# Low parts of 18 up-projection chunks: an adding DMA onto a negated copy in place of VectorE's subtraction

## The chip, the cores and the metric

The kernel runs on one core of a Trainium2 chip. The metric is device time in microseconds (us) of one execution. Before the change two timed runs gave 581.53 and 582.05 us, median 581.79.

## The reference, cut to what matters

One decoder layer on 256 tokens of width 1024, all in float32:

```python
x = layer_norm(ALPHA * x + 0.5 * swiglu(x, w_gate1, w_up1, w_down1))   # FFN 1, width 2816
h = x @ w_in + b_in                                                    # queries, keys, values, gates
y = [mixer_b(h) @ w_proj_b for b in ("sliding window", "block sparse", "memory")]
x = layer_norm(ALPHA * x + sum(sigmoid(g_b) * y_b) @ w_out)
x = layer_norm(ALPHA * x + 0.5 * swiglu(x, w_gate2, w_up2, w_down2))   # FFN 2
# swiglu(x, g, u, d) = (silu(x @ g) * (x @ u)) @ d
```

Every weight is used once per execution, so the kernel streams all of them from device memory.

## The kernel before, in words

The weights are cut into chunks of 1 MiB, each a tile `raw` of [128, 2048] float32. By `plan()` there are 96 chunks (the short description of the change says 108): 33 for each FFN, 10 for the projections of the attention, 20 for gates, output projections and `w_out`. In an FFN the gate and up chunks alternate, g0, u0, g1, u1, ... g10, u10, and the 11 down chunks follow. In FFN 1 chunk number 2c is gate c and number 2c + 1 is up c. So "chunk 5" is the up chunk c = 2, and "chunk 21" is u10.

TensorE multiplies with two parts of every number, both in the format float32r: the high part `whi` is the rounded weight, the low part `wlo` is what is missing, `raw - whi`. `split` makes them, and every chunk goes through it:

```python
def split(src, hi, lo):
    nc.scalar.copy(hi, src)                                  # L125, ScalarE
    return nc.vector.tensor_sub(lo, src, hi.bitcast(F32))    # L126, VectorE
```

Three sets of tiles carry a chunk. `raws` has 3 buffers: the load of a later chunk waits until the last reader of the buffer is done. `parts` has 4 buffers for `whi` and 4 for `wlo`: the parts of chunk i go where chunk i - 4 was, so ScalarE can begin with chunk i when TensorE has finished chunk i - 4. TensorE's sums stand in 8 banks of `ps`, two for each gate or up chunk.

For a gate or up chunk `feature_tile_2` (L201, L202) runs, for each of two halves of 128 features, 8 pairs of matmuls: `whi` against 512 columns (both parts of x side by side), then `wlo` against 256. `added` (L207, L208) copies one half of the result with ScalarE (`b`) and adds the other with VectorE into `g` or `u`. After an up chunk `gated` takes the silu on ScalarE (`s`, L342) and the product on VectorE (`h`, L344), and `split` turns it into `hh` and `hl`.

Between the chunks of FFN 1 two hooks load other inputs. The second one, at c = 7, loads `memT` (1 MiB) into a `raw` buffer and splits it as well.

The order on ScalarE, VectorE, TensorE and GpSimd is set by the scheduler of the framework from data dependences and its own estimates, and on SP (the queue that issues the loads) it is the order of the program. Each engine works through its instructions in that order, and one that waits holds up those behind it. `queue_behind` adds orderings by hand: the VectorE pieces in `lows[i]` of some chunks issue after a named instruction of the layer norms, one of them for the up chunk c = 2 of FFN 2.

Below, T5 is the time at which TensorE begins chunk 5 of FFN 1, and so on.

Of the kernel before, what the change touches and what calls it, by code (L numbers as in the profile page):

```python
# [31 lines left out]
# columns of w_in  # L32
# [3 lines left out]
def plan():  # L36
    """The weights in the order of their use, in chunks of 1 MiB: key, how it is split, and the layout
    of its [128, 2048]. All but v and the rows of down and out are 8 row tiles of 256 columns."""
# [31 lines left out]
    # query heads i and 3 + i of a share a tile  # L70
# [19 lines left out]
def vectors(d):  # L90
    """Biases by partition: 3 pairs of query heads of a, keys of a, queries and keys of b, queries of m,
    gates, keys of mem; and those by column: sinks, values of a and b, values of mem."""
    b = d["b_in"][0]
    qa = b[QA : QA + 384].reshape(2, 3, 64).transpose(1, 0, 2).reshape(3, P)
    parts = [qa, b[KA : KA + P], b[QB : QB + 768], b[QM:], d["b_mem_kv"][0, :256]]
    by_partition = np.concatenate([v.reshape(-1, P) for v in parts]).T
    by_column = np.concatenate([d["attn_sinks"][0], b[VA : VA + P], b[VB : VB + 384], d["b_mem_kv"][0, 256:]])
    return by_partition, by_column[None]


class Parts(tuple):
    """The high and the low part of a [128, tiles, 2, tokens]"""
# [7 lines left out]
def hybrid_layer(ctx: ExitStack, tc: tile.TileContext, a: dict, out: bass.AP):  # L110
# [12 lines left out]
    def split(src, hi, lo):  # L123
        """src = hi + lo exactly, both of 12 significant bits"""
        nc.scalar.copy(hi, src)  # L125
        return nc.vector.tensor_sub(lo, src, hi.bitcast(F32))  # L126

    def queue_behind(ins, others):
        """others issue after ins, on the same engine"""
        for o in others:  # L130
            tc.add_manual_dep(o.ins, ins.ins.name, mybir.DependencyInfo(mybir.DependencyClass.NoSync,
                                                                        mybir.DependencyReason.DATA))

    # ---------------------------------------------------------------- weights
# [15 lines left out]
    def part_to(n):  # L150
        while done["part"] <= min(n, len(chunks) - 1):
            i = done["part"]
            load_to(i)
            raw, how = raw_of.pop(i), chunks[i][1]
            if how:
                t = "1" if how == "leadg" else "2"
                hi = acts.tile([P, 2048], F32R, name="lhi", tag="A" + t)
                lo = acts.tile([P, 2048], F32R, name="llo", tag="B" + t)
            else:
                hi = parts.tile([P, 2048], F32R, name="whi")  # L160
                lo = parts.tile([P, 2048], F32R, name="wlo")
            # in small pieces where the engines have other work to do in time
            n_ = 512 if i < 6 or index["mk"] - 4 <= i <= index["u", 2, 3] else 2048
            lows[i] = [split(raw[:, o : o + n_], hi[:, o : o + n_], lo[:, o : o + n_]) for o in range(0, 2048, n_)]
            part_of[i] = (hi, lo)
            done["part"] += 1
# [10 lines left out]
    def product(ps, terms, first=True, last=True):  # L177
        """ps = sum of l.T @ r over terms, each a pair of parts; low times low lies below float32"""
# [14 lines left out]
    def feature_tile(ps, w, col, x, n=KD):  # L193
        """ps [128 features, 256 tokens] of a chunk's columns"""
        product(ps, [(two(w, ALL, slice(k * 256 + col, k * 256 + col + P)), two(x, ALL, k, ALL)) for k in range(n)])

    def feature_tile_2(ps, w, col, x, ks=range(KD)):
        """ps [128 features, 2 x 256 tokens], whose halves add up to the product"""
# [5 lines left out]
    def added(dst, ps):  # L204
        """dst = the sum of the halves"""
# [4 lines left out]
    def token_tile(ps, w, x, t):  # L210
        """ps [tokens of tile t, the chunk's 256 columns]"""
        product(ps, [(two(x, ALL, k, tok(t)), two(w, ALL, slice(k * 256, (k + 1) * 256))) for k in range(KD)])

    # -------------------------------------------------------------- constants
# [15 lines left out]
    def tokens_of(name):  # L230
        """both parts side by side: a product can take them in one pass"""
# [6 lines left out]
    def transposed(src, t, dst, pool=mm):  # L238
        """src [128 tokens, 1024] -> both parts [128, 8, 256 tokens], at the tokens of tile t"""
# [8 lines left out]
    def keep_warm(n):  # L248
        """the tensor engine's clock rises, and stays up, while it has work"""
# [4 lines left out]
    # x and the first two chunks, split in the order in which they come  # L254
# [28 lines left out]
    def distances():  # L283
        # Out of sight where the mask is. Query tile 0 against keys 0-127,
        # query tile 1 against keys 0-255.
# [11 lines left out]
    # ------------------------------------------------------------------- FFN  # L297
    def halves(name, tags):
        """22 feature tiles of 256 tokens, in two tiles"""
# [5 lines left out]
    def per_token(keys, lhs, keep, after, ahead=2, between=None, ends=HALVES):  # L305
        """after(t, [(start, stop, columns)]) of lhs(k, t).T @ the row tiles of weights, 2 in a chunk. The
        last keep chunks are taken by token tile, so that tile 0 ends early, and the last two by columns:
        by halves, and for tile 1 by ends."""
# [30 lines left out]
    def gated(g, u):  # L339
        """half of silu(g) * u: the layer adds half of what the FFN gives"""  # L340
# [6 lines left out]
    def ffn(n, x, after, start=0, hooks={}, h=None, ends=HALVES):  # L347
        hh, hl = h or (halves("hh", ("A1", "A2")), halves("hl", ("B1", "B2")))
        for c in range(start, NC):
# [3 lines left out]
            for key in ("g", "u"):  # L353
                w = weights((key, n, c))
                ps = [mm.tile([P, 512], F32, name="ps") for _ in range(2)]
                # the first chunks by quarters, as they come
# [11 lines left out]
    # ------------------------------------------------------------ layer norms  # L368
# [6 lines left out]
    def normalize(t, pss, resid, put, k=1.0):  # L375
        """layer norm of alpha * resid + ps / k, by the columns of pss"""
# [30 lines left out]
    # --------------------------------------------------------- FFN 1 and LN 1  # L407
# [18 lines left out]
    # keys [128 of two heads, pair, 256] and values [128 keys, key tile, heads * 64] of mem  # L426
# [3 lines left out]
    def biased(ps, bc, hi, lo):  # L430
        """hi + lo = ps + bias, by partition"""
# [23 lines left out]
    # ------------------------------------------------------------ projections  # L455
    # feature tiles of two heads: B1 q and k of b, B2 q of a, k of a, q of m
# [6 lines left out]
    # what attention gives takes the place of its queries  # L463
# [21 lines left out]
    # -------------------------------------------------------------- attention  # L485
    # A head's scores: columns 0-127 are query tile 0 against keys 0-127, the
    # rest query tile 1 against all keys. Memory: query tiles against 256 keys.
# [6 lines left out]
    def scores(nm):  # L494
        """8 times the scores, and their softmax"""
# [4 lines left out]
        for e in range(0, n, 2):  # L500
            # two heads in turn, in the two halves of the rows
# [44 lines left out]
    def turn(nm, i):  # L546
        """the probabilities of a pair's heads with keys on partitions: keys 0-127, then 128-255"""
# [14 lines left out]
    def weigh(nm, i):  # L562
        """values [128 keys, two heads] against the probabilities of both"""
# [12 lines left out]
    # Twice a sigmoid is 1 + tanh of half its argument: the gates hold the tanh,  # L576
    # mixed is twice what the layer mixes, and the layer norm halves the sum.
# [51 lines left out]
    # ------------------------------------------------------ mix, W_out, LN 2  # L629
# [35 lines left out]
    # ----------------------------------------------------------- FFN 2, LN 3  # L665
    # The first chunks by token tile, so that tile 0 runs while tile 1 is normalized.
# [61 lines left out]
```

## Time and profile before

| | |
|---|---|
| timed runs | 581.53 and 582.05 us, median 581.79 us |
| span of the profiled execution (first to last instruction) | 580.4 us |
| what a timed run has beyond that span | 1.1 to 1.7 us |
| TensorE (PE) busy | 569.9 us, 98% of the span |
| VectorE (DVE) busy | 393.0 us, 68% |
| ScalarE (ACT) busy | 305.1 us, 53% |
| GpSimd (POOL) busy | 23.5 us, 4% |
| DMA engines busy, mean of 16 | some 52% of the span |

Busy time says how much work an engine had, not whether it set the end. A matmul's busy time overlaps with that of its neighbours. The profile names what ended each wait of an engine, and the chain of work that ended last; both are read below for the stretches that the change touches.

### The profile page before, as it was taken

The numbers are of one execution on the slowest core, as the hardware profiler recorded it, in microseconds if no ns is written. First come the engines' busy times: TensorE is split into PE (matmuls) and PEld (weight loads), VectorE is DVE, ScalarE is ACT, GpSimd is POOL, SyncE is SP. The second block draws the span as 40 slices with busy tenths as digits, with TensorE's granted clock in tenths as the row PEclk, the third lists the DMA queues.
The fourth block names the chain that finished last, engine by engine and source line by source line (L and its number), as shares of the span: only waits on it lengthen the run. The fifth ranks groups of instructions, "written<-read, shape, count | busy, mean of one in ns | idle before, by whom it ended". The sixth has DMA issues, their size and how long they took to land.

```text
span 580.4 us, 9070 instructions
## 1 busy us (share of the span) xinstructions
PE 569.9 (98%) x3634; PEld 514.3 (89%) x3634; DVE 393.0 (68%) x594; ACT 305.1 (53%) x528; POOL 23.5 (4%) x37
## 2 busy tenths in 40 slices
PE   8999999999999999999999999999999999999994
PEld 7888888888888998999999999889988888888884
DVE  5877667665446977698887566995557666663336
ACT  6865656644433653965965454633565645543300
POOL 2000000000000000000002012210000000000001
PEclk9999999999999999999999999999999999999998
DMA  8895747745543384094162554537454545546101
GB/s 274 313 322 226 272 152 289 265 164 217 213 165 131 146 290 145 14 350 147 62 230 88 204 212 151 217 146 256 180 177 186 213 154 213 194 169 218 73 0 72
DMA packets 18025, 108.99 MB, mean 188 GB/s; under 512 B 2112, under 2 KB 2368, under 8 KB 5696
## 3 DMA queue, kind: packets, MB, share of 16 engines
q1 hardware_dynamic: 17984, 108.43, 51.6%
q8 instruction: 28, 0.46, 0.3%
q14 instruction: 13, 0.11, 0.1%
HBM read 107.37 MB, written 1.05 MB: 187 GB/s over the span
## 4 chain that ended last, share of the span: by engine, by line
PE 93%; ACT 3%; DVE 2%; DMA 1%; issue 0%; POOLq 0%; SPq 0%; DVEq 0%
PE ps L201 25%; PE ps L182 18%; PE ps L181 18%; PE ps L183 17%; PE ps L202 13%; ACT whi L125 1%; DMA raw<-in_w_dram 1%; ACT sc_b L531 1%; PE ps L555 1%; PE ps L244 1%; DVE sc_b L515 0%; DVE m L520 0%; PE ps L508 0%; ACT gates L589 0%; DVE r L399 0%
## 5 line engine op out<-in xcount | busy, mean ns | idle before, releaser
L126 DVE TENSOR_TENSOR wlo<-raw,whi 128x512 fp32r<-128x512 f32 (+1 forms) x232 | 233.3, 1039 | 134.1 <-ACT whi L125 133.7
L125 ACT CAST whi<-raw 128x512 fp32r<-128x512 f32 (+1 forms) x232 | 196.2, 888 | 143.9 <-PE ps L183 58.3
L201 PE MATMUL ps<-x0T,whi 128*128 128x512 f32 x352 | 123.4, 396 | 1.2 <-ACT whi L125 0.7
L201 PE MATMUL ps<-x2T,whi 128*128 128x512 f32 x288 | 100.2, 394 | 0.0
L202 PE MATMUL ps<-x0T,wlo 128*128 128x256 f32 x352 | 97.9, 282 | 0.0
L181 PE MATMUL ps<-x1T,whi 128*128 128x256 f32 x288 | 82.3, 286 | 0.3 <-ACT sc_m L531 0.3
L182 PE MATMUL ps<-x1T,whi 128*128 128x256 f32 x288 | 81.5, 283 | 0.0
L183 PE MATMUL ps<-x1T,wlo 128*128 128x256 f32 x288 | 81.5, 283 | 0.0
L201 PEld LDWEIGHTS ps<-x0T,whi 128*128 128x128 f32 x352 | 66.4, 190 | 16.1 <-ACT whi L125 2.1
L202 PE MATMUL ps<-x2T,wlo 128*128 128x256 f32 x288 | 79.9, 277 | 0.0
L182 PE MATMUL ps<-wlo,hh 128*128 128x512 f32 (+1 forms) x198 | 72.5, 366 | 0.0
L181 PE MATMUL ps<-whi,hh 128*128 128x512 f32 (+1 forms) x198 | 72.5, 366 | 0.0
L183 PE MATMUL ps<-whi,hl 128*128 128x512 f32 (+1 forms) x198 | 72.4, 365 | 0.0
L202 PEld LDWEIGHTS ps<-x0T,wlo 128*128 128x128 f32 x352 | 67.2, 191 | 0.6
L201 PEld LDWEIGHTS ps<-x2T,whi 128*128 128x128 f32 x288 | 54.0, 188 | 12.6
L181 PEld LDWEIGHTS ps<-x1T,whi 128*128 128x128 f32 x288 | 55.2, 192 | 0.8 <-ACT sc_m L531 0.5
L182 PEld LDWEIGHTS ps<-x1T,whi 128*128 128x128 f32 x288 | 55.2, 192 | 0.0
L183 PEld LDWEIGHTS ps<-x1T,wlo 128*128 128x128 f32 x288 | 55.2, 192 | 0.0
L202 PEld LDWEIGHTS ps<-x2T,wlo 128*128 128x128 f32 x288 | 54.1, 188 | 0.0
L181 PEld LDWEIGHTS ps<-whi,hh 128*128 128x128 f32 x198 | 37.3, 188 | 6.2
L183 PEld LDWEIGHTS ps<-whi,hl 128*128 128x128 f32 x198 | 37.3, 188 | 6.1
L182 PEld LDWEIGHTS ps<-wlo,hh 128*128 128x128 f32 x198 | 37.3, 188 | 6.0
(167 smaller groups left out, 715.1 us busy)
## 6 DMA issues: line engine op xcount, KB each, us to landing
raw<-in_w_dram SPq DMA_DIRECT2D x92, 1024.0 KB, 4.8
raw<-in_w_dram SPq DMA_DIRECT2D x16, 256.0 KB, 5.4
ln<-in_ln_dram SPq DMA_DIRECT2D x3, 1024.0 KB, 6.8
xT<-in_xT_dram SPq DMA_DIRECT2D x4, 256.0 KB, 6.6
x_sb<-in_x_dram SPq DMA_DIRECT2D x1, 1024.0 KB, 7.1
raw<-in_memT_dram SPq DMA_DIRECT2D x1, 1024.0 KB, 5.2
out_dram<-r SPq DMA_DIRECT2D x3, 256.0 KB, 2.0
brow<-in_by_column_dram SPq DMA_DIRECT2D x1, 387.0 KB, 8.0
```

The source lines that it names most:

```text
L125: nc.scalar.copy(hi, src)
L126: return nc.vector.tensor_sub(lo, src, hi.bitcast(F32))
L181: nc.tensor.matmul(ps, lh, rh, start=first and i == 0, stop=False)
L182: nc.tensor.matmul(ps, lh, rl, start=False, stop=False)
L183: nc.tensor.matmul(ps, ll, rh, start=False, stop=last and i == n - 1)
L201: nc.tensor.matmul(ps, wh, x.both[:, k], start=k == 0, stop=False)
L202: nc.tensor.matmul(ps[:, S:], wl, x[0][:, k], start=False, stop=k == KD - 1)
L244: nc.tensor.transpose(ps[:, j * P : (j + 1) * P], src[:, k * P : (k + 1) * P], ident)
L531: nc.scalar.activation(sc[:, e, c0:c1], raw[e][:, c0:c1], AF.Exp, bias=negm[:, e, t : t + 1], scale=SCALE, accum_out=ssum[:, e, t : t + 1])
L555: nc.tensor.transpose(pt[:, s * n + j * P : s * n + (j + 1) * P], sc[:, 2 * i + s, c : c + P], ident)
```

## The change: what it does

For the up chunks with c from 2 to 10 of both FFNs (18 chunks) the low part is made in another way. ScalarE writes `whi` as before, in one piece of 2048 columns, then a second time the negated, rounded weight into `wlo`. GpSimd then issues a DMA that adds `raw` onto `wlo`, so that `wlo` ends as `raw - whi`. VectorE has no part in it. The list `lows` of such a chunk is empty, so the ordering by hand for the up chunk c = 2 of FFN 2 is gone. The diff without changes to comments:

```diff
-            n_ = 512 if i < 6 or index["mk"] - 4 <= i <= index["u", 2, 3] else 2048
-            lows[i] = [split(raw[:, o : o + n_], hi[:, o : o + n_], lo[:, o : o + n_]) for o in range(0, 2048, n_)]
+            key = chunks[i][0]
+            if key[0] == "u" and key[2] >= 2 and not how:
+                nc.scalar.copy(hi, raw)
+                nc.scalar.activation(lo, raw, AF.Copy, scale=-1.0)
+                nc.gpsimd.dma_start(out=lo, in_=raw, accum_op=ALU.add)
+                lows[i] = []
+            else:
+                n_ = 512 if i < 6 or index["mk"] - 4 <= i <= index["u", 2, 3] else 2048
+                lows[i] = [split(raw[:, o : o + n_], hi[:, o : o + n_], lo[:, o : o + n_]) for o in range(0, 2048, n_)]
```

In the rows that follow, a name ends in the number of its buffer, and the line numbers after the change are 8 higher from `split`'s callers on. First ScalarE's queue where chunk 5 (`raw_197`) is split, before and after; `raw_199` is chunk 6, `raw_252` chunk 7.

```order
L207 COPY b_361<-ps_324 128x256
L125 CAST whi_366<-raw_197 128x512 x4
L207 COPY b_411<-ps_376 128x256
L125 CAST whi_425<-raw_199 128x2048
L207 COPY b_414<-ps_377 128x256
L342 ACTIVATE s_417<-g_357 128x512
L125 CAST whi_472<-raw_252 128x2048
```

```order
L215 COPY b_361<-ps_324 128x256
L165 CAST whi_366<-raw_197 128x2048
L166 ACTIVATE wlo_367<-raw_197 128x2048
L215 COPY b_406<-ps_371 128x256
L125 CAST whi_420<-raw_199 128x2048
L215 COPY b_409<-ps_372 128x256
L350 ACTIVATE s_412<-g_357 128x512
L165 CAST whi_467<-raw_252 128x2048
L166 ACTIVATE wlo_468<-raw_252 128x2048
```

The four casts of chunk 5 have become one cast and the negated copy, back to back; chunk 7 has its negated copy behind its cast.

Next ScalarE's queue at an up chunk in the middle of FFN 1, chunk 15 (`raw_693` before, `raw_690` after); the copies `b` around it are those of chunks 13 and 14.

```order
L207 COPY b_834<-ps_799 128x256
L125 CAST whi_895<-raw_693 128x2048
L207 COPY b_837<-ps_800 128x256
L342 ACTIVATE s_840<-g_786 128x512
L207 COPY b_887<-ps_852 128x256
L125 CAST hh0_181<-h_842 128x512
```

```order
L215 COPY b_833<-ps_798 128x256
L165 CAST whi_894<-raw_690 128x2048
L215 COPY b_836<-ps_799 128x256
L350 ACTIVATE s_839<-g_784 128x512
L166 ACTIVATE wlo_895<-raw_690 128x2048
L125 CAST hh0_181<-h_841 128x512
L215 COPY b_886<-ps_851 128x256
```

The negated copy stands behind the copy `b` and the silu that follow the cast, and ahead of `hh`.

Last ScalarE's queue at the end of FFN 1's up chunks: `raw_892` is chunk 19, `raw_947` is `memT`, `raw_951` chunk 20, `raw_998` chunk 21. Only the queue after the change is shown; before it, the cast of `memT` stood ahead of the cast of chunk 19.

```order
L165 CAST whi_1101<-raw_892 128x2048
L215 COPY b_1043<-ps_1006 128x256
L350 ACTIVATE s_1046<-g_991 128x512
L166 ACTIVATE wlo_1102<-raw_892 128x2048
L125 CAST memT0_176<-raw_947 128x2048
L125 CAST hh1_182<-h_1048 128x512
L215 COPY b_1093<-ps_1058 128x256
L125 CAST whi_1155<-raw_951 128x2048
L215 COPY b_1096<-ps_1059 128x256
L215 COPY b_1141<-ps_1106 128x256
L215 COPY b_1144<-ps_1107 128x256
L350 ACTIVATE s_1147<-g_1092 128x512
```

The cast of `memT` has moved behind the negated copy of chunk 19; the cast of chunk 21, two `hh` and `b` instructions and its negated copy follow the last of these rows. On GpSimd nine DMA instructions now stand between the building of the distance tables and the first layer norm, and nine more between the second and the third. On SP the load of `memT` waits for the adding DMA of chunk 17, and the load of chunk 21 for VectorE's part of `memT`, whose buffer it takes.

## Rows read from the trace of the kernel before

**Rows 1.** The page: an engine's busy time and share; the granted clock in 40 slices.

```profile
PE 569.9 (98%) x3634; PEld 514.3 (89%) x3634; DVE 393.0 (68%) x594; ACT 305.1 (53%) x528; POOL 23.5 (4%) x37
PEclk9999999999999999999999999999999999999998
```

**Rows 2.** Busy time by stretch: length, then each engine; clock, DMA share, GB/s.

```profile
41.75:52.84 11.09, 11.09 (x66) 9.78 (x65) 7.31 (x8) 6.16 (x8) 0.00 (x0) 1.00 0.47 182
63.94:130.50 66.56, 66.56 (x386) 58.69 (x385) 45.94 (x49) 38.66 (x50) 0.00 (x0) 1.00 0.61 221
416.00:516.00 100.00, 100.00 (x578) 87.39 (x577) 65.06 (x71) 55.55 (x72) 0.00 (x0) 1.00 0.53 190
```

**Rows 3.** Waits of all engines: who waited for whom, total, times, longest.

```profile
DVE wlo L126 <- ACT whi L125: 133.7, 73, 5.7
...
ACT whi L125 <- PE ps L201: 44.1, 20, 2.6
...
PEld ps L201 <- ACT whi L125: 2.1, 2, 1.4
```

**Rows 4.** ScalarE in order of time, 26 to 37 us: start, length, what, wait before.

```profile
26.36 0.37 ACT L207 COPY b<-ps 128x256 f32<-128x256 f32 x1
26.62 2.19 ACT L125 CAST whi<-raw 128x512 fp32r<-128x512 f32 x4
...
29.41 1.91 ACT L125 CAST whi<-raw 128x2048 fp32r<-128x2048 f32 x1 [0.34 <-DMA raw<-in_w_dram]
...
36.20 1.92 ACT L125 CAST whi<-raw 128x2048 fp32r<-128x2048 f32 x1 [0.77 <-PE ps L201]
```

**Rows 5.** ScalarE in order of time, two chunks in the middle of FFN 1.

```profile
41.75 1.91 ACT L125 CAST whi<-raw 128x2048 fp32r<-128x2048 f32 x1 [2.22 <-PE ps L201]
43.56 0.36 ACT L207 COPY b<-ps 128x256 f32<-128x256 f32 x1
43.82 0.63 ACT L342 ACTIVATE s<-g 128x512 f32<-128x512 f32 x1
...
52.84 1.91 ACT L125 CAST whi<-raw 128x2048 fp32r<-128x2048 f32 x1 [2.28 <-PE ps L201]
```

**Rows 6.** VectorE in order of time at the same place.

```profile
43.69 2.29 DVE L126 TENSOR_TENSOR wlo<-raw,whi 128x2048 fp32r<-128x2048 f32 x1 [2.58 <-ACT whi L125]
45.90 0.42 DVE L208 TENSOR_TENSOR u<-ps,b 128x256 f32<-128x256 f32 x1
46.42 0.69 DVE L344 SCALAR_TENSOR_TENSOR h<-u,s 128x512 f32<-128x512 f32 x1
```

**Rows 7.** The page's DMA issues: transfer, queue, count, size, median us from issue to landing.

```profile
raw<-in_w_dram SPq DMA_DIRECT2D x92, 1024.0 KB, 4.8
```

**Rows 8.** DMA view, 74 to 107 us: GB/s in 40 slices.

```profile
GB/s 0 60 278 417 417 99 0 159 60 437 447 179 10 0 0 149 308 427 447 417 447 397 387 417 367 50 0 0 79 209 407 457 219 199 387 467 308 447 407 219
```

**Rows 9.** SP's queue in order of time: the load of memT.

```profile
90.39 0.33 SPq L419 DMA_DIRECT2D raw<-in_memT_dram  x1
```

**Rows 10.** ScalarE in order of time, 95 to 120 us.

```profile
95.62 1.92 ACT L125 CAST memT<-raw 128x2048 fp32r<-128x2048 f32 x1 [0.68 <-DMA raw<-in_memT_dram]
...
108.31 1.91 ACT L125 CAST whi<-raw 128x2048 fp32r<-128x2048 f32 x1 [2.22 <-PE ps L201]
...
110.38 0.63 ACT L342 ACTIVATE s<-g 128x512 f32<-128x512 f32 x1
...
113.71 0.62 ACT L125 CAST hh<-h 128x512 fp32r<-128x512 f32 x1 [2.13 <-DVE h L344]
114.23 0.37 ACT L207 COPY b<-ps 128x256 f32<-128x256 f32 x1
...
119.40 1.91 ACT L125 CAST whi<-raw 128x2048 fp32r<-128x2048 f32 x1 [2.28 <-PE ps L201]
```

**Rows 11.** VectorE in order of time: its part of memT.

```profile
97.57 2.29 DVE L126 TENSOR_TENSOR memT<-raw,memT 128x2048 fp32r<-128x2048 f32 x1 [0.68 <-ACT memT L125]
```

**Rows 12.** ScalarE in order of time, the start of FFN 2's up chunks.

```profile
395.79 1.07 ACT L125 CAST x2T<-ps 128x512 fp32r<-128x512 f32 x2
...
416.14 1.91 ACT L125 CAST whi<-raw 128x2048 fp32r<-128x2048 f32 x1 [2.37 <-PE ps L201]
```

## The prediction

> **What bounds the kernel now.** I began with the busy times and the granted clock [rows 1]. TensorE is busy 569.9 of the span's 580.4 us, at the full of its two clock levels in all but the last slice. A busy share is an average, so the next view was the busy time by stretch, for the gate and up chunks that the change touches [rows 2]: there TensorE is busy 11.09 of 11.09 us, 66.56 of 66.56 and 100.00 of 100.00. It never waits; two chunks take 11.09 us, one 5.55. VectorE has 7.3 us of work in those 11.09, ScalarE 6.2. The waits say the same from the other side [rows 3]: VectorE waits 133.7 us in all for ScalarE's casts, ScalarE 44.1 us for TensorE to free a buffer of parts, and the one wait of weight loading for a cast is 2.1 us, at the start. So the work that the change takes away stands beside a full TensorE, and the question is only whether the low parts still come in time.
>
> The time lines give the dates for that. ScalarE's cast of chunk i waits for TensorE to end chunk i - 4, so the casts that end a wait for TensorE mark borders between chunks: T5 = 36.20 [rows 4], T6 = 41.75 and T8 = 52.84 [rows 5], T18 = 108.31 and T20 = 119.40 [rows 10]; the rest follow at 5.55 us, T21 = 124.95 among them. In the middle of FFN 1 the cast of chunk 9 starts at T6 and VectorE's part ends at 43.69 + 2.29 = 45.98 [rows 6]; TensorE wants it at T9 = 58.4, 12.4 us later. That cover is what the change spends.
>
> **VectorE's part that goes.** 18 chunks at 2.29 us [rows 6], 41 us, all of it behind TensorE: 0 on the path. No gain hides there: TensorE's whole idle time is 580.4 - 569.9 = 10.5 us, and in the stretches concerned it is none [rows 2].
>
> **ScalarE's part that comes.** 18 passes over 2048 columns at 1.91 us, the price of the cast [rows 5]. Per pair of chunks ScalarE goes from 6.2 to 8.1 of 11.1 us. The copies behind it come up to 2 us later, which the 8 banks cover (a chunk takes two). If that cover were gone, a pass would cost its 1.91 us. On the path to the low part it counts in full.
>
> **The adding DMA.** Call X the time from the end of the negated copy to the landing of the sum. The trace has no such transfer, and no DMA from GpSimd. The nearest row is a load of the same 1 MiB: 4.8 us from issue to landing [rows 7]; X can hardly be less. Of that, data: in 416 to 516 us the engines were 0.53 busy for 190 GB/s [rows 2], 53 us for 18.1 MiB, 2.9 us per MiB; at the best rate seen, 467 GB/s [rows 8], 2.2 us. That leaves 1.9 to 2.6 us fixed. An add has to read two operands: with no load beside it, 2.6 + 4.4 = 7.0 to 1.9 + 5.8 = 7.7 us. But loads go on all the time, one per 5.55 us. With one of them shared in, 2.6 + 3 x 2.2 = 9.2 to 1.9 + 3 x 2.9 = 10.6; with two, 11.4 to 13.5. I take X = 9.9, the middle of the case with one load, since the add is about as long as one to two chunks and shares the engines with what comes in between. Bounds: 4.8 and, if two loads and a write that doesn't overlap the reads (one more 2.9) come together, 16.
>
> The Trainium skill (Collectives: The Full Stack, "The bandwidth ceiling: the fold count and why AG ≠ RS ≠ AR") says that an add inside a DMA costs no cycles of its own but a second read, which halves the rate of about 31 GB/s per engine. An estimate from that page is 16 x 15.5 = 248 GB/s, 4.2 us for 1 MiB; with 1.9 to 2.6 us fixed that is some 6.5 us and would make the whole change cost about 1 us. No row here shows an add.
>
> **Where the cover is thin.** Three cases, in order of time, each a budget for X.
>
> 1. Chunk 5. Its cast starts at 26.62 [rows 4]; two passes end at 26.62 + 3.8 = 30.4; T5 is 36.20. Budget 5.8 us. TensorE stalls X - 5.8 = 4.1 us, once. Chunk 7 has 9.8 us and moves with that stall: 0.
>
> 2. The steady case (chunks 9 to 19 of FFN 1, and all of FFN 2 from u4). Cast at T(n-3), then copy b and silu, then the negated copy: 1.91 + 0.36 + 0.63 + 1.91, less 0.1 to 0.2 of overlap, so 4.6 us after T(n-3) [rows 5]. TensorE comes 16.65 us after it: budget 12.1. At X = 9.9 nothing stalls. Above 12.1 every other up chunk does (its parts lie where the up chunk two before it lay, so one stall covers the next): some 7 stalls in both FFNs. In FFN 2 the first sum has more: the x2T casts end at 396.9, the negated copy at 398.8, u2 starts at 416.14 [rows 12], 17.3 us. The ordering by hand that goes there concerned VectorE's pieces, which are gone too.
>
> 3. Chunk 21, behind memT. SP's load of memT, issued at 90.39 [rows 9], now waits for the add of chunk 17, which starts at T14 + 4.6 = 90.7, so it is issued at 90.7 + X and lands 5.2 later (as 90.39 to 95.62, [rows 9, 10]). Its cast stands behind chunk 19's negated copy, which ends at T16 + 4.6 = 101.8; 1.92 us [rows 10], then VectorE 2.29 [rows 11], then the load of chunk 21 into that buffer, 4.8 [rows 7], then cast, hh, b and negated copy, 1.91 + 0.62 + 0.37 + 1.91 = 4.8 [rows 10], then X. The sum is the later of 115.6 + X and 109.7 + 2X, against T21 = 124.95. Stall: the larger of X - 9.35 and 2X - 15.25. At 9.9 that is 4.6 us. In FFN 2 no memT stands in the way.
>
> Behind GpSimd's adds only other adds and, long after, the layer norm are queued; behind SP's later loads stand the loads of the next chunks, which the two cases above have in them.
>
> **Sum.** 4.1 + 4.6 = 8.7 us on a span of 580.4, which makes 589.1. The timed runs lie 1.1 to 1.7 us above the span, with the median at 581.8, so I predict 590.5.
>
> **Rivals.** What a measurement can tell from no change is about 2%, 11.6 us; X = 10.9 is that point.
>
> *Hidden anyway.* X is no more than 7, the loads don't disturb it: 581.8 to 583. For it: a short SBUF to SBUF path, and the page's estimate above. Against: the case of chunk 5 asks for 5.8 even so, and loads fill half the DMA time. 12%.
>
> *The adds are slow (the other side).* One mechanism: an add beside two loads, or with a dearer start from GpSimd's queue than SP's. Place: chunks 5 and 21 first, from 12.1 on every other up chunk. X = 12 costs 6.2 + 8.8 = 15.0: 597. X = 14: 8.2 + 12.8 + 7 x 1.9 = 34: 616. X = 16: 54: 636. It decides from 10.9. For it: bounds above reach it without strain. Against: the best rates of rows 8 show room. 30%.
>
> *The DMA engines become the bound.* Two loads and two reads per pair of chunks are 4 x 2.9 = 11.6 us against 11.1: 0.5 us more per pair, 9 us on 18 pairs beside the stalls above, 600; with the write counted too, 14.5 us per pair, 61 us, 640. Against: at 2.2 us per MiB four are 8.8. 11%.
>
> *VectorE holds the add up.* At T6 + 4.6 VectorE runs pieces of 0.42 to 0.69 us [rows 6]; if the add's start waits one out, X is 10.6 and the time 592; behind one of 2.29, 12.2 and 598. The Trainium skill (SBUF — State Buffer, "SBUF: two separate sides") warns that GpSimd cannot write descriptors while VectorE runs in a two-port mode. The subtraction's 2.29 us for 2048 columns is about one column per cycle of the 0.96 GHz that the skill gives, so no such mode shows here. 3%.
>
> *Faster, or not what it says.* Nothing for TensorE to gain, 1%. The order of instructions shows 9 + 9 adds on GpSimd, so the change does what it says.
>
> **How the numbers follow.** The forecast (X from 7 to 10.9, 583 to 593.4) has 43%. Same: 43 + 12 + 2 (of VectorE's) = 57%; slower 30 + 11 + 1 = 42%; faster 1%. The range leaves out the bottom of "hidden" (about 6%) and the top of the two slow cases (about 13%): 582.5 to 625.
>
> **What would show it.** A wait of TensorE of 3 to 6 us at T5 and of about as much at T21, for the adding DMA; none at chunks 9 to 19 and in FFN 2; X by the time to landing of GpSimd's DMA, 8.5 to 11; DMA share in gate and up stages near 0.9; VectorE's idle time up by some 40 us; granted clock still full. It is wrong if X is over 12 (waits at every other up chunk), if the clock falls after a stall, or if ScalarE's later copies hold TensorE at the banks.

## The result, and the profile after

The changed kernel takes 618.11 us (median of 616.5 and 619.72) against 581.79 before: 1.061 times the time, 95% interval 1.058 to 1.064. It is slower by 36 us, where the prediction said 8.7. In one experiment below (half of the gate chunks loaded) one of four runs took 897.68 us at a granted clock of 0.587, and its median is that of the other three.

The page of the changed kernel: an engine's busy time, the granted clock in 40 slices, the DMA queues (packets, MB, share of 16 engines; q0 is GpSimd's), and the DMA issues with their median time to landing.

```profile
PE 578.4 (94%) x3634; PEld 517.0 (84%) x3634; DVE 352.9 (57%) x567; ACT 333.3 (54%) x537; POOL 39.2 (6%) x55
...
PEclk9989999989999999999999999999999999999998
...
q1 hardware_dynamic: 17984, 108.43, 48.7%
q0 software_dynamic: 2592, 18.88, 15.2%
...
raw<-in_w_dram SPq DMA_DIRECT2D x92, 1024.0 KB, 4.9
wlo<-raw POOLq DMA_DIRECT2D x18, 1024.0 KB, 10.7
```

Against [rows 1], VectorE has lost the 40 us that the change takes from it and ScalarE has gained 28. TensorE does the same 3634 matmuls, yet is busy 8.5 us longer. The clock row has two slices below the 9 where it had none before the last. An add takes 10.7 us at the median, not far from the 9.9 of the prediction. The waits of the changed kernel (who waits for whom: us, times, longest) say where the rest is.

```profile
ACT whi L125 <- DMA raw<-in_w_dram: 40.5, 21, 5.9
ACT whi L165 <- DMA raw<-in_w_dram: 36.9, 11, 5.3
...
PE ps L210 <- DMA wlo<-raw: 25.4, 12, 4.4
```

TensorE now waits 25.4 us for adds, 12 times, where [rows 3] have no wait of TensorE for a low part. The span is 614.7 us, 34.3 longer: 25.4 of it are these waits; the other 8.9 are nearly all TensorE's longer busy time (8.5 us). The second line is the key: the cast of an up chunk (L165) waits for its load, 36.9 us in all. In [rows 3] and [rows 5] it waited for TensorE.

TensorE in order of time, seven of its eight waits for an add in FFN 1 (start, length, what, wait before): chunks 5, 9, 11, 13, 15, 19 and 21.

```profile
39.99 0.58 PE L210 MATMUL ps<-x0T,wlo 128*128 128x256 f32 x1 [3.72 <-DMA wlo<-raw]
...
64.33 0.39 PE L210 MATMUL ps<-x0T,wlo 128*128 128x256 f32 x1 [0.20 <-DMA wlo<-raw]
...
77.70 0.38 PE L210 MATMUL ps<-x0T,wlo 128*128 128x256 f32 x1 [1.79 <-DMA wlo<-raw]
...
91.09 0.39 PE L210 MATMUL ps<-x0T,wlo 128*128 128x256 f32 x1 [1.82 <-DMA wlo<-raw]
...
105.90 0.39 PE L210 MATMUL ps<-x0T,wlo 128*128 128x256 f32 x1 [3.45 <-DMA wlo<-raw]
...
135.51 0.58 PE L210 MATMUL ps<-x0T,wlo 128*128 128x256 f32 x1 [4.35 <-DMA wlo<-raw]
...
150.91 0.39 PE L210 MATMUL ps<-x0T,wlo 128*128 128x256 f32 x1 [2.53 <-DMA wlo<-raw]
```

The waits that were forecast are there: 3.72 at chunk 5, 2.53 at chunk 21. The ones between them were not: six, 13.7 us with chunk 17's 2.12. FFN 2 has four more, 5.4 us.

The chain of work that ended last shows why (start, length, what). From 31 to 119 us it runs through the two DMA queues and ScalarE, and never through TensorE:

```profile
31.42 8.52 DMA wlo<-raw
...
39.96 11.87 DMA raw<-in_w_dram
...
51.90 4.23 issue
...
56.14 8.15 DMA wlo<-raw
...
64.31 9.45 DMA raw<-in_w_dram
...
73.82 4.86 issue
...
78.69 12.35 DMA wlo<-raw
...
91.52 9.40 DMA raw<-in_w_dram
```

Read the dates. The add of chunk 5 lands at 31.42 + 8.52 = 39.94; at 39.96 the load of chunk 9 starts, since it takes the raw buffer that the add has read. It runs beside the add of chunk 7 (issued at 39.10) and takes 11.87 us, where a load took 4.8 [rows 7]. Chunk 9's cast can start only then, and the two passes and the issue take to 56.14; its add lands at 64.29, and at 64.31 the load of chunk 13 starts. This passing of a raw buffer from an add to the next load is called the hand-over below, and load, two passes and add together the loop. The same cast in ScalarE's time line of the changed kernel:

```profile
51.85 1.91 ACT L165 CAST whi<-raw 128x2048 fp32r<-128x2048 f32 x1 [3.97 <-DMA raw<-in_w_dram]
```

From load to load this loop takes 64.31 - 39.96 = 24.4 us, then 27.2. It serves every fourth chunk, and TensorE needs 4 x 5.55 = 22.2 us for four. That is the steady loss: 2 to 5 us for four chunks. On TensorE it shows as waits and, behind some of them, as time at the lower clock.

### The profile page after: what moved, and what is told of

Its sections match the earlier page's. It is cut to its first block, busy times and chain, and to the rows that moved or that the text cites. A ratio compares the mean times of both kernels' runs of the same rounds, so it can differ in the third digit from the quotient of the medians.

```text
span 614.7 us, 9112 instructions
## 1 busy us (share of the span) xinstructions
PE 578.4 (94%) x3634; PEld 517.0 (84%) x3634; DVE 352.9 (57%) x567; ACT 333.3 (54%) x537; POOL 39.2 (6%) x55
## 3 DMA queue, kind: packets, MB, share of 16 engines
q1 hardware_dynamic: 17984, 108.43, 48.7%
q0 software_dynamic: 2592, 18.88, 15.2%
HBM read 107.37 MB, written 1.05 MB: 176 GB/s over the span
## 4 chain that ended last, share of the span: by engine, by line
PE 59%; DMA 26%; issue 6%; ACT 5%; DVE 2%; SPq 1%; POOLq 0%; DVEq 0%; ACTq 0%
PE ps L190 16%; PE ps L189 16%; PE ps L191 16%; DMA raw<-in_w_dram 13%; DMA wlo<-raw 11%; PE ps L209 5%; PE ps L210 3%; ACT whi L125 1%; DMA raw<-in_memT_dram 1%; ACT sc_b L539 1%; ACT wlo L166 1%; PE ps L563 1%; PE ps L252 1%; ACT b L215 0%; DVE sc_b L523 0%
## 5 line engine op out<-in xcount | busy, mean ns | idle before, releaser
L126 DVE TENSOR_TENSOR wlo<-raw,whi 128x512 fp32r<-128x512 f32 (+1 forms) x205 | 191.4, 966 | 132.0 <-ACT whi L125 131.7
L125 ACT CAST whi<-raw 128x512 fp32r<-128x512 f32 (+1 forms) x205 | 161.0, 829 | 130.0 <-PE ps L191 56.2
L209 PE MATMUL ps<-x0T,whi 128*128 128x512 f32 x352 | 128.0, 406 | 2.0 <-DVE x0T L126 1.2
L210 PE MATMUL ps<-x0T,wlo 128*128 128x256 f32 x352 | 100.7, 290 | 20.0 <-DMA wlo<-raw 20.0
L210 PEld LDWEIGHTS ps<-x0T,wlo 128*128 128x128 f32 x352 | 68.7, 195 | 23.4 <-DMA wlo<-raw 22.6
L209 PEld LDWEIGHTS ps<-x0T,whi 128*128 128x128 f32 x352 | 67.9, 194 | 18.6 <-ACT whi L125 3.2
L165 ACT CAST whi<-raw 128x2048 fp32r<-128x2048 f32 x18 | 34.4, 1909 | 48.2 <-DMA raw<-in_w_dram 36.9
## 6 DMA issues: line engine op xcount, KB each, us to landing
wlo<-raw POOLq DMA_DIRECT2D x18, 1024.0 KB, 10.7
```

What stands on the lines that cost most here:

```text
L165: nc.scalar.copy(hi, raw)
L209: nc.tensor.matmul(ps, wh, x.both[:, k], start=k == 0, stop=False)
L210: nc.tensor.matmul(ps[:, S:], wl, x[0][:, k], start=False, stop=k == KD - 1)
```

## The experiments

Four theories were set against each other. A: the add holds the raw buffer, so that the load after it is late. B: the DMA engines are too full. C: ScalarE's extra pass is in the way. D: an add is that long in itself. The experiments stand by question, not in the order of time. All times are medians; the ratio is to the kernel before on the same chip, with its 95% interval. Diffs are against the changed kernel unless said otherwise.

**ScalarE's extra pass alone.** The negated copy stays, VectorE subtracts over it.

```diff
-                nc.gpsimd.dma_start(out=lo, in_=raw, accum_op=ALU.add)
-                lows[i] = []
+                lows[i] = [nc.vector.tensor_sub(lo, raw, hi.bitcast(F32))]
```

> The changed kernel with VectorE's subtraction put back for the 18 chunks and no adding DMA; ScalarE still writes the negated copy, which the subtraction then overwrites. Both theories (raw buffers held by the adds; DMA engines too full for the adds) put the loss on the DMA, so 581 to 584 us. If ScalarE's extra 18 passes or their place in its queue carried the loss, 600 us or more.

582.42 us, 1.0007 [0.9991, 1.0024]. The extra pass costs nothing, as predicted; all of the loss comes with the DMA.

**One add alone.** Chunk 13 of FFN 1, the other 17 back to VectorE.

```diff
-            if key[0] == "u" and key[2] >= 2 and not how:
+            if key[0] == "u" and key[1] == 1 and key[2] == 6 and not how:
```

> One add alone, in FFN 1 at c = 6, the other 17 chunks by VectorE. Theory B: X of 8 to 10.5 us (it shares with one or two loads, but no second add or late load is queued), no wait of TensorE: 581.5 to 583. Theory D: X of 10.5 or more, still no wait under 12.1: the same time, so here the time to landing decides.

581.76 us, 0.9993 [0.998, 1.0006]. The page's DMA issues of this run:

```profile
wlo<-raw POOLq DMA_DIRECT2D x1, 1024.0 KB, 7.1
```

So an add is not long in itself (theory D): 7.1 us, under the 8 expected. No load ran beside it: from its issue at 68.65 us to its landing the DMA engines moved its 1 MiB and nothing else. It is the company of other transfers, loads or adds, that makes most adds of the changed kernel 8 to 14.

**Which adds, and how many.** One FFN or the other, every second add, and half the columns of each.

```diff
# e_ffn1, e_ffn2, e_odd: the condition has in addition
+ key[1] == 1        + key[1] == 2        + key[2] % 2
# e_half
+                nc.scalar.activation(lo[:, 1024:], raw[:, 1024:], AF.Copy, scale=-1.0)
+                nc.gpsimd.dma_start(out=lo[:, 1024:], in_=raw[:, 1024:], accum_op=ALU.add)
+                lows[i] = [nc.vector.tensor_sub(lo[:, :1024], raw[:, :1024], hi[:, :1024].bitcast(F32))]
```

> Only the 9 chunks of FFN 1 get the adding DMA. From TensorE's waits for adds in the changed kernel (20.0 us in FFN 1, 5.4 in FFN 2) and the share of the lower clock: 606 to 612 us. If the FFNs lost alike (the adds too slow everywhere), 600 us.

> Only the 9 chunks of FFN 2 get the adding DMA. By TensorE's waits in the changed kernel 587 to 592 us; if the FFNs lost alike, 600 us. Together with the run on FFN 1 the losses should add up to the 36 us of the changed kernel.

> Only the up chunks with odd c (3, 5, 7, 9) of both FFNs, 8 adds instead of 18. Raw buffers held by the adds in a chain, in which one add starts the load whose chunk's add starts the next load: with every second add gone the chain has slack in between, 582 to 588 us. A fixed price for each add: 36 x 8 / 18 = 16 us, 598 us.

> The 18 chunks with half of the columns (1024) by negated copy and adding DMA and the other half by VectorE's subtraction. An add of 0.5 MiB should land 5 to 7.5 us after its issue instead of 10.7. Raw buffers held by the adds: loads start some 4 us earlier, the chain fits, 582 to 588 us. A price for each add whatever its size: 605 us or more.

FFN 1's nine: 605.24 us, 1.039 [1.036, 1.043]. FFN 2's nine: 589.34, 1.012 [1.009, 1.015]. Odd c, eight adds: 588.61, 1.009 [1.006, 1.012], one wait of 2.81 us, add 7.9 us at the median. Half the columns: 593.64, 1.019 [1.017, 1.022], two waits, of 2.19 and 7.68 us near memT. Nine adds in FFN 1 cost some 23 us, nine in FFN 2 only 7 (together 30 of the 36), eight at every second up chunk of both 5 to 6: the cost is not by the piece. Why FFN 2 loses so much less was not taken apart; [rows 2] have a DMA share of 0.61 in FFN 1 and of 0.53 in FFN 2. With half the columns TensorE waits for no add before chunk 17, as the hand-over would have it; the two waits near memT are what misses the 582 to 588.

**The raw buffer set free.** The add reads the weights in device memory, so the buffer is free after the negated copy; or a fourth raw buffer (and a control for the smaller work pool that makes room for it).

```diff
# e_hbm
-                nc.gpsimd.dma_start(out=lo, in_=raw, accum_op=ALU.add)
+                nc.gpsimd.dma_start(out=lo, in_=a["w"][i], accum_op=ALU.add)
# e_w4r4 (e_w4 has the second line alone; in both the tile idle moves into work)
-    raws = ctx.enter_context(tc.tile_pool(name="raws", bufs=3))
+    raws = ctx.enter_context(tc.tile_pool(name="raws", bufs=4))
-    work = ctx.enter_context(tc.tile_pool(name="work", bufs=6))
+    work = ctx.enter_context(tc.tile_pool(name="work", bufs=4))
```

> The changed kernel, but the adding DMA reads the weights from device memory and not from the raw tile, so a raw buffer is free as soon as ScalarE's two passes are done. If the loss is the raw buffer that an add holds and the load that waits for it, most of it goes: 585 to 595 us, TensorE's waits for adds 3 to 10 us instead of 25.4. If the adds are late because the DMA engines are too full, the traffic is the same: 612 us or more.

> The changed kernel with four raw buffers instead of three (and four work tiles instead of six, which makes the room). Raw buffers held by the adds: the load that waits for an add has one chunk (5.5 us) more, 588 to 600 us. DMA engines too full: 612 us or more, since the same bytes move.

> The control for the run with four raw buffers: the changed kernel with four work tiles instead of six and three raw buffers. Both theories: 616 to 622 us, as the changed kernel.

610.54 us, 1.049 [1.045, 1.053]; 607.12, 1.043 [1.040, 1.046]; the control 612.96, 1.053 [1.049, 1.057]. The control missed its 616 to 622 by 3 us. The first run gives back 8 us, the second 6 against its control; both are short of what theory A asked for by the totals. The waits of the run with four buffers say more:

```profile
ACT whi L165 <- DMA raw<-in_w_dram: 9.4, 2, 6.6
...
PE ps L210 <- DMA wlo<-raw: 15.5, 6, 5.0
```

With all loads in place, the fourth buffer takes most of the casts' wait for loads away (9.4 us, where the changed kernel has 36.9 and the control 24.4), as the hand-over would have it; TensorE keeps 15.5 us of waits for adds, of which 2.07 at chunk 5 and 4.99 near memT. In the run from device memory the waits are others: 18.9 us in six, and 14.6 of that are two, 7.58 at chunk 5 and 7.05 near memT; from chunk 7 to the place of memT there is none. An add from device memory took 12.4 us at the median, which is dear where the cover is thin.

**Without the two thin places.** The adds of chunk 5 and chunk 21 go back to VectorE; then the same with the adds from device memory.

```diff
# e_mid; e_mid_hbm has in addition in_=a["w"][i] in the add
-            if key[0] == "u" and key[2] >= 2 and not how:
+            if key[0] == "u" and 2 + (key[1] == 1) <= key[2] <= 10 - (key[1] == 1) and not how:
```

> 16 adds are left: those of FFN 1 for c = 3 to 9 and those of FFN 2 for c = 2 to 10; the two with thin covers in my prediction (chunk 5, and chunk 21 behind memT) go back to VectorE. The prediction's steady case (parts are in time whenever the add takes under 12.1 us) gives 582 to 584, no wait for an add. Theory A (the load of an up chunk waits for the add of an earlier up chunk that holds its raw buffer, and load and add make each other longer, so that two up chunks take over 22.2 us) keeps the waits of chunks 9 to 19 and of FFN 2: in the run with all 18 adds these were about 14 us in FFN 1 and 5 in FFN 2; less the clock, 596 to 604. Theory B (the DMA engines are simply full) gives the same 596 to 604, since two adds less change little; the next run separates A from B.

> The same 16 adds, but each reads the weights in device memory in place of raw, so no raw buffer is held; the traffic of the DMA engines is the same in bytes. Theory A gives 582 to 588, no waits for adds in the middle of FFN 1. Theory B gives the time of the run before within 4 us (596 to 604), and loads that still take 8 us or more beside an add. The prediction's steady case gives 582 to 584.

603.01 us, 1.034 [1.031, 1.038], and 605.31, 1.040 [1.035, 1.046]. By the totals A fell, since the run from device memory is no faster, but the waits of TensorE differ in kind. From raw, FFN 1 has 1.19, 2.19, 1.45 and 4.73 us at chunks 11, 13, 15 and 17. From device memory (TensorE in order of time):

```profile
49.39 0.39 PE L210 MATMUL ps<-x0T,wlo 128*128 128x256 f32 x1 [0.73 <-DMA wlo<-in_w_dram]
...
72.83 0.39 PE L210 MATMUL ps<-x0T,wlo 128*128 128x256 f32 x1 [0.98 <-DMA wlo<-in_w_dram]
...
96.07 0.39 PE L210 MATMUL ps<-x0T,wlo 128*128 128x256 f32 x1 [0.77 <-DMA wlo<-in_w_dram]
...
126.47 0.58 PE L210 MATMUL ps<-x0T,wlo 128*128 128x256 f32 x1 [7.93 <-DMA wlo<-in_w_dram]
```

Three waits of under a microsecond, every other up chunk: with adds of 11.6 to 13.1 us (median 12.6) in this stretch, that is about what the prediction's budget of 12.1 gives. The 7.93 is another matter: here the scheduler put the cast of memT ahead of that of chunk 19 on ScalarE, which waited 7.85 us for memT's load.

**Traffic and held buffers without an add on TensorE's path.** The kernel before, with plain DMAs from GpSimd to a place in device memory that nobody reads: of both parts, or twice of raw.

```diff
# against the kernel before; e_hold has (raw, raw)
+            key = chunks[i][0]
+            if key[0] == "u" and key[2] >= 2:
+                for j, t_ in enumerate((lo, hi)):
+                    nc.gpsimd.dma_start(out=a["scratch"][key[1] - 1, 2 * (key[2] - 2) + j], in_=t_)
# left out here: the declaration of scratch
```

> The kernel before (VectorE subtracts) with plain DMAs from GpSimd that copy both parts of the same 18 up chunks, 2 x 1 MiB each, to a place in device memory that nobody reads; TensorE waits for none of them, but parts buffers are free only when the copy has landed. It is as much DMA engine time as the adds (2 x 2.9 us of all engines a chunk against 5.2) without an add on the path. If full DMA engines alone make the change slow (theory B): loads of 7 us or more and 592 to 610. If it is that TensorE's low part comes through the add: loads slower, but under the cover of 12 us, 582 to 586.

> The kernel before with two plain DMAs from GpSimd of each such up chunk's raw to that place: the raw buffer is held until they land, as by the add, and the traffic is the same as in the run before; TensorE still waits for VectorE's low part alone. Theory A in its pure form (held buffer and slow loads): the load of the next up chunk comes late, TensorE waits for casts, 588 to 600. If the add itself on the path to the low part is needed too (cast, negated copy, then add, one after the other): 582 to 586, since load and cast alone fit under four chunks of 22.2 us.

588.37 us, 1.009 [1.007, 1.011], and 597.3, 1.026 [1.019, 1.033]. Waits of the second run:

```profile
PE ps L205 <- ACT whi L125: 10.9, 4, 7.8
PE ps L206 <- DVE wlo L126: 3.4, 2, 1.8
...
SPq L147 <- DMA scratch_dram<-raw: 116.0, 16, 14.8
```

With the same load on the DMA engines, holding the raw buffer costs 9 us more than not holding it. Now it is TensorE's casts that are late, behind loads that wait for the copies, though no low part comes by DMA. The first run fits neither expectation: the traffic alone costs 5 to 6 us, with two waits for VectorE's parts in FFN 1 (4.60 and 1.63 us) and loads there of 9.8 us at the median. So plain copies beside a load lengthen it as well; it does not take an add.

**Less load traffic.** Of each gate chunk from c = 2 only a quarter, or half, is loaded; its casts and subtractions read that part several times over, so the result is not the reference's.

```diff
+            for o in range(0, 512 if light(i) else 2048, min(n_, 512) if light(i) else n_):
+                m_ = min(n_, 512) if light(i) else n_
+                nc.sync.dma_start(out=raw_of[i][:, o : o + m_], in_=a["w"][i][:, o : o + m_])
# left out here: the function light (gate chunks with c >= 2 of both FFNs), the lines replaced, the split that reads 512 columns four times
```

> The changed kernel with all 18 adds; of the gate chunks from c = 2 only a quarter (512 of 2048 columns) is loaded, and the casts and subtractions read it four times over, so the weights of these chunks are not the reference's; buffers, waits and the work of the engines stay. The DMA engines have 2.9 + 0.7 + 5.2 = 8.8 us of work in 11.1 where they had 11.0. Theory B (add and load are long because they share full DMA engines): adds of 7.5 to 9 us, no wait in the steady stretch, a wait of 2 to 3 us at chunk 5 and at most 3 near chunk 21: 583 to 590. Theory D (an add is that long in itself): adds of 10 us or more, waits as in the changed kernel: above 600.

> The same with half of these gate chunks (1024 of 2048 columns) loaded: 2.9 + 1.45 + 5.2 = 9.6 us of work in 11.1. Theory B: between the run with a quarter and the changed kernel, adds of 8.5 to 10.5 us, 588 to 602. Theory D: above 605.

609.89 us, 1.046 [1.044, 1.049], and 616.54, 1.057 [1.054, 1.061]. Theory B fell as a bound on the average: taking 2.2 of 11 us of engine time out of every pair of chunks gave back 8 us, where 583 to 590 was expected. The chain of the run with a quarter shows the same loop:

```profile
31.16 7.67 DMA wlo<-raw
...
38.84 10.21 DMA raw<-in_w_dram
...
49.12 4.80 issue
...
53.94 6.92 DMA wlo<-raw
```

The add of chunk 5 lands, the load of chunk 9 starts that instant and takes 10.21 us, beside the add of chunk 7, issued at 37.60. The gate loads that are gone were never in this loop. It is the hand-over itself that puts a load and an add side by side. While their data move, the DMA engines are full: the share falls to 0.04 only in the last 2.3 us before the landing of chunk 9's load at 51.83. Busy time by stretch (length, PE, weight loads, VectorE, ScalarE, GpSimd; clock, DMA share, GB/s), two such stretches of the changed kernel and the one of this run:

```profile
39.96:49.50 9.54, 9.51 (x47) 8.26 (x48) 4.12 (x7) 3.09 (x4) 0.00 (x1) 0.85 0.96 276
64.31:73.82 9.51, 9.48 (x54) 8.28 (x55) 3.98 (x5) 3.02 (x5) 0.88 (x1) 1.00 0.94 275
```

```profile
38.84:49.05 10.21, 10.18 (x58) 8.87 (x59) 2.97 (x4) 2.55 (x3) 0.00 (x0) 1.00 1.01 248
```

So B is right within a hand-over, where the share is 0.94 to 1.01, and wrong as a bound for the whole.

**The loop given room.** The light gate chunks get two small tiles of their own, so that the three raw buffers pass among up chunks alone and a buffer comes round after six chunks, 33.3 us, in place of four, 22.2; then also without the adds of chunks 5 and 21; and the light loads with adds from device memory.

```diff
+    small = ctx.enter_context(tc.tile_pool(name="small", bufs=2))
-            raw_of[i] = raws.tile([P, 2048], F32, name="raw")
+            raw_of[i] = small.tile([P, 512], F32, name="few") if light(i) else raws.tile([P, 2048], F32, name="raw")
# left out here: what makes the gate chunks light, and the smaller work pool of e_w4
```

> The run with a quarter of the gate loads, all 18 adds, and these gate chunks in two small tiles of their own (512 columns), so that the three raw buffers pass among up chunks alone: the load of chunk n waits for the add of chunk n - 6 in place of n - 4 (the work pool has 4 buffers in place of 6, which by itself moved the changed kernel by less than 1%). Loop theory (the load waits for an add, runs beside the next add, and its late cast makes the add after it late): no wait for loads in the steady stretch and no steady stalls; left are chunk 5 (2 to 3 us) and the place of memT and chunk 21 (3 to 6 us): 585 to 593. If the adds are late for another reason (engines or GpSimd's queue): still 600 or more, waits of 1 to 3 us at up chunks 11 to 17.

> The same without the adds of chunk 5 and chunk 21 (VectorE makes those). Loop theory: nothing is left that stalls, 582 to 585. Otherwise 595 or more.

> A quarter of the gate loads, the three raw buffers as in the changed kernel, but the adds read the weights in device memory: the raw buffer is free after ScalarE's negated copy. Loop theory: the load doesn't wait for an add, no waits in the steady stretch as long as an add takes under 12.1 us; the adds were 12.4 to 12.7 us from device memory with all loads, with fewer loads 9 to 12: 584 to 594 with the waits at chunk 5 and chunk 21. Otherwise 600 or more.

588.85 us, 1.010 [1.007, 1.014], and 587.63, 1.007 [1.005, 1.009]: of the 28 us that the light run still lost, 21 are gone. The smaller work pool is part of this edit; alone it gave the changed kernel 5 us (612.96 for 618.11), so some 16 of the 21 at least are the loop's. The first of them, its waits, its adds in FFN 1 (20 to 165 us: shortest, median, longest to landing), and ScalarE's casts of up chunks in order of time:

```profile
PE ps L221 <- DMA wlo<-raw: 6.2, 3, 3.1
```

```profile
DMA to landing us min/median/max: 8.3/11.4/12.4
```

```profile
44.99 1.91 ACT L171 CAST whi<-raw 128x2048 fp32r<-128x2048 f32 x1 [2.28 <-PE ps L220]
...
56.08 1.91 ACT L171 CAST whi<-raw 128x2048 fp32r<-128x2048 f32 x1 [2.28 <-PE ps L220]
...
78.91 1.91 ACT L171 CAST whi<-raw 128x2048 fp32r<-128x2048 f32 x1 [2.28 <-PE ps L220]
...
90.01 1.91 ACT L171 CAST whi<-raw 128x2048 fp32r<-128x2048 f32 x1 [2.28 <-PE ps L220]
```

Busy time by stretch from 45 to 100 us, the changed kernel and then this run:

```profile
45.00:100.00 55.00, 51.18 (x289) 43.84 (x288) 20.65 (x29) 32.55 (x37) 3.43 (x4) 1.00 0.90 267
```

```profile
45.00:100.00 55.00, 54.63 (x316) 47.91 (x315) 22.31 (x32) 36.25 (x41) 4.27 (x5) 1.00 0.91 249
```

This is the telling run. The adds are no shorter: 11.4 us at the median, more than in the changed kernel. The DMA engines are as busy, 0.91 for 0.90. But the casts wait for TensorE again, 2.28 us as in [rows 5], and the steady stretch has one wait, of 0.37 us. Left are 3.06 us at chunk 5 and 2.72 near memT. The run without the adds of chunks 5 and 21 missed its 582 to 585 by a little; its two waits are 1.05 us at chunk 9 and 2.03 near memT.

The run from device memory took 605.75 us, 1.037 [1.034, 1.041], where 584 to 594 was expected. TensorE's waits in it, in order of time, are only three:

```profile
42.63 0.58 PE L220 MATMUL ps<-x0T,wlo 128*128 128x256 f32 x1 [4.28 <-DMA wlo<-in_w_dram]
...
131.19 0.58 PE L220 MATMUL ps<-x0T,wlo 128*128 128x256 f32 x1 [7.59 <-DMA wlo<-in_w_dram]
...
517.28 0.39 PE L220 MATMUL ps<-x2T,wlo 128*128 128x256 f32 x1 [2.12 <-DMA wlo<-in_w_dram]
```

Between the waits at chunk 5 and chunk 19 TensorE waits for no add, over 81 us, so the expectation for the steady stretch held. What missed was the price of the ends: chunk 5 with an add of 10.5 us, chunk 19 behind memT's late cast, and a lower clock behind both (0.50 from 42.6 to 46 and from 131.2 to 135 us).

## Why the prediction was wrong

**The step that failed is the steady case's first date, and behind it the term for the load.** The prediction put the cast of chunk n at T(n-3), when TensorE frees the parts, as [rows 5] show for the kernel before. Budget and price followed: 12.1 us against 9.9, so no stall. The budget itself fits the runs from both sides, with adds of 11.4 us at the median and one wait of 0.37 (light loads, own tiles), and adds of 12.6 us with waits of 0.7 to 1.0 at every other up chunk (from device memory). But the date moved. The add is a reader of raw and holds its buffer until it lands, and the load that follows in that buffer starts beside the next add. The prediction charged memT's load for exactly this hand-over in step 3 and left it out of the steady case, although it says that the later loads are in both.

The hand-over alone would have been harmless: by the prediction's own terms the loop is 4.6 for the passes, 9.9 for the add and 4.8 for the load, 19.3 us, and four chunks take 22.2. The term that broke it is the load at 4.8 us; beside an add it took 9.4 to 11.9, so that the cast waited for it, and the loop measured 24.4 and 27.2 us. The prediction shared the engines between an add and a load when it worked out X, and left the load as long as if it were alone. Charged by the same rule the load is also 9.9, and the loop 24.4 us, above 22.2. That sum was made afterwards, and that it meets the first measured turn to the tenth is luck, since the parts of that turn were 11.9, 4.3 and 8.2.

The time lies within the range of 582.5 to 625, but in the part that was there for the slow rivals.

**What it cost.** Of the 34.3 us of span, 19.1 are the ten waits for which the prediction had 0: 13.7 in FFN 1, 5.4 in FFN 2. Another 8.9 are no waits for adds, and it had 0 for them too; the prediction named a falling clock as what would make it wrong, without a price. Behind the waits at chunks 5, 19 and 21 four or five pairs of matmuls each (`whi`, then `wlo`) start 0.64 us apart in place of 0.35, which by an estimate from these spacings is some 4 of the 8.9; the rest was not taken apart. The two waits that it had, 8.7 us, measured 6.3.

**Chunk 5** has the right place, and 3.72 us for 4.1 is in part luck. The negated copy ended at 31.10 and not at 30.4, and TensorE wanted the sum at 36.27, so the budget was 5.2 us for 5.8; and the sum landed at 39.94, an X of 8.8 for 9.9.

**Chunk 21** has the right place and 2.53 us for 4.6. Earlier stalls had moved TensorE by then, memT's load took 7.26 us for 5.2 and chunk 21's add 7.68 for 9.9, so the term was not measured by itself; taking both adds out saved 15 us of 618, clock and followers with them.

**X** was estimated well: 10.7 us at the median for 9.9 (7.4 to 13.7), and 7.1 with no load beside it for 7.0 to 7.7. The estimate from the Trainium skill (Collectives: The Full Stack, "The bandwidth ceiling: the fold count and why AG ≠ RS ≠ AR"), about 6.5 us, is near the add alone. Its halved rate shows roughly as well: 15.2% of 614.7 us for 18 adds are 5.2 us of all engines each, where a load has 48.7% for 108.43 MB, 2.9 us a MiB, a factor of 1.8.

**The rivals.** The slow adds had the right side and a part in the loss. Six of the 18 adds took more than 12.1 us, four of them in FFN 1, up to 13.7; what they exceed 12.1 by is, as an estimate, some 5 of the 19.1 us of unforeseen waits. The rest are late casts, and the place was not every other up chunk but each from 9 to 21. DMA engines as the bound on the average fell with the light loads (610 us) and the own tiles (589 us at a share of 0.91), though traffic alone costs 5 to 6. That VectorE holds an add up did not show in the one add that ran by itself: VectorE worked beside it, and it took 7.1 us. ScalarE's pass cost nothing, as stated.

**What stays open.** That a load and an add side by side take about 10 us fits an estimate from the rows: 5.2 + 2.9 = 8.1 us of all engines, full in these stretches, and the 1.9 to 2.6 us that the prediction found fixed make 10.0 to 10.7. Adds of 12 to 14 us have more beside them than this sum, and were not taken apart. With all loads in place the loop was only loosened, by the fourth buffer, and its cost there is not separated from that of the thin places; the proof by own tiles is with light loads. None of these versions beats the kernel before, since TensorE was full and the change can only hide.

## What to carry to other kernels

When a new reader is put on a buffer, follow the buffer past that reader: the load that takes its place now starts when the reader ends, beside the reader's next instance, and at the duration that it has there. Close the loop (load, passes, reader) and compare its length with the time that the bound engine needs for as many chunks, and when two transfers share the engines, charge the sharing to both; a budget counted from a release of the old kernel is worth nothing once the release is another. And run one instance alone before believing a time for many: one add was free, eighteen cost 36 us.

## What the runs showed of the hardware

- A load and an adding DMA side by side stretch each other well beyond their own times: a load has 4.8 us at the median in the kernel before and 9.4 to 11.9 beside an add; an add 7.1 us with nothing beside it, up to 13.7 in the changed kernel. Plain copies from GpSimd's queue did the same to loads (9.8 us at the median in FFN 1).
- A wait of TensorE can cost more than its length. In the changed kernel the matmuls behind the wait of 3.72 us run at the lower of the two clock levels (1.2 of 2.4 GHz): pairs 0.64 us apart from 39.99 to 42.3, then 0.35. The length of the wait alone does not decide it: behind the 3.45 us at chunk 15 the clock stayed full, and behind the 2.53 us at chunk 21 it fell. Busy time by stretch, columns as above, behind chunks 5, 15 and 21:

```profile
39.99:42.30 2.31, 2.31 (x8) 2.02 (x9) 0.69 (x3) 0.00 (x0) 0.00 (x0) 0.50 1.00 316
105.90:110.00 4.10, 4.10 (x23) 3.59 (x24) 1.03 (x2) 0.38 (x2) 0.80 (x1) 1.00 0.68 188
153.00:156.00 3.00, 3.00 (x12) 2.57 (x12) 0.66 (x1) 2.17 (x2) 0.00 (x0) 0.58 1.01 418
```
